# Down projection of an f32 encoder layer: pairs of k tiles, part of them by seven block products

## The chip, the core and the metric

The kernel runs on one core of a Trainium2 chip. The metric is device time in microseconds (us) for one execution of the whole layer; times given as "before" are of the unchanged kernel.

## The reference

One post-norm encoder layer on 256 tokens of width 2048, all in float32: a layer norm, one projection to 6144 columns, two kinds of attention over the 256 tokens, an output projection, and a gated feed-forward block of width 5632. What the change touches is the last line but one:

```
h = layer_norm(x, ln_in_g, ln_in_b)
proj = einsum('bsd,de->bse', h, w_in)                       # 2048 -> 6144, split in six
mixed = einsum('bse,ed->bsd', concat([na_out, diff_out]), w_out)
h = layer_norm(ALPHA * h + mixed, ln1_g, ln1_b)
ffn = einsum('bsf,fd->bsd', silu(h @ w_gate) * (h @ w_up), w_down)   # w_down: 5632 x 2048
h = layer_norm(ALPHA * h + ffn, ln2_g, ln2_b)
```

## The kernel before

**Arithmetic.** Each f32 matrix product is made of three matmuls in the format fp32r: every operand x is split in hi (x rounded, an ACTIVATE of ScalarE) and lo (x minus hi, a subtraction of VectorE), and the product is hi*hi + hi*lo + lo*hi. So each 128 x 1024 tile of weights costs one load (512 KB, SyncE's queue), one split on ScalarE and one on VectorE, and TensorE's matmuls are 128 x 128 by 128 x 512.

**Stages.** The work is a list of units, one tile of 128 rows (k) of a weight matrix and 1024 columns each. In order: six groups of 16 units for w_in; two groups of 16 for w_out ("o", 0 and 1); one chunk of 512 gate and up columns ("f", 10); five times a group "g" (gate) and a group "u" (up) of 16 units, for 1024 columns each; and ("d", 0) and ("d", 1), 44 units each, for the two halves of w_down's columns. The tokens are two tiles of 128, t = 0 and 1.

**Two kinds of steps.** Most groups go unit by unit: `mm_step(t, u)` (line 379) adds 6 matmuls for one token tile into two accumulators, a PSUM bank of 128 x 512 each. The groups g and u go by pairs of units. A pair is a 2 x 2 block matrix (two k tiles by two column halves of 512) times the 2 x 2 blocks of the tokens, so 8 block products of 3 matmuls each. In four of the eight pairs of a group (`SEVEN`) only 7 block products are taken, on sums of the blocks, in the manner of Strassen and Winograd: `seven_parts` (line 946) makes the sums of the weights (four adds of 512 columns on VectorE) and splits them, and `more_forms` (line 540) makes the sums of the tokens once, when layer norm 1 ends, since all ten groups use the same tokens. `products` (line 1008) lists the block products with their accumulators, 1 to 7; `take_product` (line 1055) issues them and reads accumulators out at the group's end.

**The down projection before** goes unit by unit, each unit 12 matmuls, 1056 in all, with four accumulators open at a time. Its left operand mid, silu(gate) * up, is transposed block by block (`mid_side`, line 905: four transposes of TensorE, a copy by ScalarE into the ring nb of two buffers, a store of 256 KB by GpSimd's queue to mid_d in HBM), read back as chunks of four k tiles (512 KB) and split (`mid_hi`, `mid_lo`, lines 914 and 918). The last eight units' part for t = 1 is kept for the end (`last_steps`, line 1248): those 48 matmuls run while the normalization of t = 0 is finished.

**What sets the order.** All engines' programs are written once, on the host, by a planner. `Timed` (line 63) keeps a clock for each engine and a time for each piece of a tile; before each step the planner looks at a window of coming steps (20 for products, 7 for others), and emits the splits and sums whose inputs its clocks call ready (`next_part`, line 1290); attention, norms and transposes are side tasks that are let in where the clocks see room (`Side`, line 177). Tiles of 4 KB a partition come from one pool of 46 slots (`slot`, line 267); PSUM banks come from `Banks` (line 140). Each engine runs its program in order, and waits at an instruction until the engines or DMAs it depends on have got there. All instructions are recorded by one helper, so the profile puts them on one line, L50.

Of the kernel before, what the change touches and what calls it, by code (L numbers as in the profile page):

```python
# [37 lines left out]
SEVEN = (0, 2, 4, 6)  # L38

# [23 lines left out]
class Timed:  # L63
# [32 lines left out]
    def note(self, name, op, outs, ins):  # L96
# [4 lines left out]
        if op == "dma_start":  # L101
# [5 lines left out]
            if name == "pool":  # L107
                end += 2.0
# [20 lines left out]
        self.clock[name] = end  # L129
        for w, r, c in map(self.times, ins):  # L130
            r[c] = np.maximum(r[c], end)
        for w, r, c in map(self.times, outs):
            w[c] = end + self.LATENCY[name]
# [6 lines left out]
class Banks:  # L140
# [30 lines left out]
    def next_idle(self):  # L171
        if self.count < 8:
            return 0.0
        return min([self.nc.idle(b) for b in self.left + self.passing], default=0.0)
# [73 lines left out]
def layer_kernel(ctx: ExitStack, tc: tile.TileContext, A: dict, out: bass.AP):  # L248
# [16 lines left out]
    slots = dict(used=0, left=[])  # L265

    def slot(shape, dt=F32):
        t = slab.tile(shape, dt, tag="slab", name=nm("sl"))
        if slots["used"] < SLOTS:
            slots["used"] += 1  # L270
        elif slots["left"]:
            old = min(slots["left"], key=lambda x: nc.idle(x))
            slots["left"].remove(old)
            nc.follows(t, old)
        return t

    def leave(*tiles):

        slots["left"] += tiles
# [33 lines left out]
    def add_group(name, ks, srcs, lhs):  # L313
        for i, k in enumerate(ks):
            units.append(dict(group=name, k=k, first=i == 0, last=i == len(ks) - 1, srcs=srcs, lhs=lhs))
# [15 lines left out]
    for j in range(NSG):  # L331
        for name, w in (("g", W_G), ("u", W_U)):
            add_group((name, j), range(KT), [w[:, j * 1024 : (j + 1) * 1024]], h1T)
    for c in range(2 * NSG, NFC - 1):
        add_f(c)
    for n in range(2):
        add_group(("d", n), range(KF), [W_D[:, n * 1024 : (n + 1) * 1024]], mid)
# [6 lines left out]

    def load(u):
        if u >= U:
            return
        if u == U - KF - 10:
# [4 lines left out]
        if units[u]["group"] == ("d", 0) and units[u]["k"] % 4 == 0:  # L353
            c = units[u]["k"] // 4
            side.drain_until(lambda: have.get(("mid whole", c), 0) == 2)
            mid_whole[c] = slot([P, 2, 4, P])
            nc.sync.dma_start(mid_whole[c], mid_d[c * P : (c + 1) * P, :])
        r = slot([P, 1024])
# [20 lines left out]
    def mm_step(t, u):  # L379
# [14 lines left out]
        if t == 1:  # L394
            leave(hi, lo)

# [21 lines left out]
    AHEAD_S = 20  # L418
    NPRE = 7
    NPRE_S = 8  # L420

# [54 lines left out]
    def ln_side(key, t, g, b, store, tiles, n_whole):  # L476
# [10 lines left out]
        for c in range(4):  # L487
            while (key, t, c, "norm") not in have:
                yield None
            yield "pe", [chunk(h[t], c)]  # L490
# [34 lines left out]
    def part_split(key, t, c, f, parts, late):  # L525
# [7 lines left out]
        have[key, t, c] = 1  # L533

# [3 lines left out]
    hF, forms, halves = {}, {}, []  # L538

    def more_forms(i):  # L540
# [12 lines left out]
        else:  # L553
            n = 2
            f = ring("s", 4, (P, 4, P))
            nc.vector.tensor_tensor(f[:, :2], ab, cd, op=ALU.subtract)
        f = f[:, :n]
        if n == 4:
            parts = slot([P, 2, n, P], F32R)
        elif len(halves) % 2 == 0:  # L560
            halves.append(slot([P, 2, 2, 2, P], F32R))
            parts = halves[-1][:, 0]
# [88 lines left out]
    def setup():  # L651
# [14 lines left out]
        nc.vector.tensor_copy(diag, bk[:DF_H, :])  # L666
        diag_d = dram.tile([DF_H, 512], F32, name="diag_d")
# [10 lines left out]
        nc.vector.tensor_tensor(lp, lv[:, 0:4:2, :], lv[:, 1:4:2, :], op=ALU.mult)  # L678
        ls = const.tile([P, 2], F32, name="ls")
# [28 lines left out]
    def qk_side(name, t, nat):  # L708
        for n in range(2):
# [7 lines left out]
            have[name] = have.get(name, 0) + 1  # L717

# [45 lines left out]
    def diff_head(hd):  # L764
# [29 lines left out]
        for qt in range(2):  # L794
            for kt in range(2):
# [6 lines left out]
                )  # L802
        o = ring("o", 2)
# [45 lines left out]
    def na_head(hd):  # L849
# [36 lines left out]
        for kt in range(2):  # L886
# [6 lines left out]
            )  # L893
        j = hd // 4
# [8 lines left out]
    mid_whole = {}  # L903
# [13 lines left out]

    def mid_lo(c):
        hi, lo = mid_tiles[c]
        nc.vector.tensor_tensor(lo, mid_whole[c], hi.bitcast(F32), op=ALU.subtract)  # L920
        leave(mid_whole[c])
# [11 lines left out]
    def op(engine, fn, reads=(), after=()):  # L933

        return dict(engine=engine, fn=fn, reads=reads, after=after, done=False)

    def one_parts(u):
# [6 lines left out]
        return [op("act", lambda: split_hi(u), lambda: [raw[u]]), op("dve", lo, lambda: [wh[u]], (0,))]  # L944

    def seven_parts(u):
# [23 lines left out]
        def lo13():  # L970
            nc.vector.tensor_tensor(s["lo"], s["t"], s["hi"].bitcast(F32), op=ALU.subtract)

        def t24():
            s["u"] = slot([P, 2, 512])
            nc.vector.tensor_tensor(s["u"][:, 0], s["t"][:, 0], r2[:, 512:], op=ALU.add)
            nc.vector.tensor_tensor(s["u"][:, 1], s["u"][:, 0], r2[:, :512], op=ALU.add)

# [4 lines left out]
        def lo24():  # L982
            nc.vector.tensor_tensor(s[4], s["u"], s[2].bitcast(F32), op=ALU.subtract)
            leave(s["u"], s["t"])

        def lo2():
            split_lo(u + 1)
            leave(r2)

        return [  # L990
            op("act", hi11, lambda: [r1]),
# [432 lines left out]
```

## Time and profile before

| | us |
|---|---|
| median of 3 runs (1129.63 to 1130.07) | 1130.06 |
| the profiled execution | 1130.14 |
| span of the profiled execution | 1128.2 |
| TensorE busy in the span | 1116.9 |
| VectorE busy | 848.6 |
| ScalarE busy | 569.9 |
| down projection, first matmul to its last accumulator | 875.5 to 1116.5 |

Times in rows are counted from the start of the span. PE is TensorE, PEld its weight loads, DVE VectorE, ACT ScalarE, POOL GpSimd, SP SyncE. "busy" counts an engine's instructions; idle time before an instruction stands in brackets, with what ended it. A tile's name in a row is that of the program without its number: sl is a slot, acc a PSUM bank, nb the ring of copies, s and o other rings.

### The profile page before, as it was taken

The numbers are of one execution on the slowest core, as the hardware profiler recorded it, in microseconds if no ns is written. First come the engines' busy times: TensorE is split into PE (matmuls) and PEld (weight loads), VectorE is DVE, ScalarE is ACT, GpSimd is POOL, SyncE is SP. The second block draws the span as 40 slices with busy tenths as digits, with TensorE's granted clock in tenths as the row PEclk, the third lists the DMA queues.
The fourth block names the chain that finished last, engine by engine and source line by source line (L and its number), as shares of the span: only waits on it lengthen the run. The fifth ranks groups of instructions, "written<-read, shape, count | busy, mean of one in ns | idle before, by whom it ended". The sixth has DMA issues, their size and how long they took to land.

```text
span 1128.2 us, 13969 instructions
## 1 busy us (share of the span) xinstructions
PE 1116.9 (99%) x5064; PEld 911.8 (81%) x5064; DVE 848.6 (75%) x1110; ACT 569.9 (51%) x740; POOL 60.3 (5%) x111
## 2 busy tenths in 40 slices
PE   8999999999999999999999999999999999999997
PEld 4788887888888867888888888888888888888885
DVE  7863867446774579899999999999999663455435
ACT  5552556325474236655566566555656543435420
POOL 2000003020100020000000000000000000000001
PEclk9999999999999999999999999999999999999999
DMA  9865548697857764564765766755757976567621
GB/s 328 274 186 157 158 149 178 210 180 187 180 166 276 239 195 153 184 219 170 249 214 189 246 205 216 227 191 210 238 190 277 350 248 240 183 244 234 224 67 74
DMA packets 68611, 234.24 MB, mean 208 GB/s; under 512 B 8388, under 2 KB 8516, under 8 KB 68544
## 3 DMA queue, kind: packets, MB, share of 16 engines
q1 hardware_dynamic: 63216, 217.61, 57.4%
q0 software_dynamic: 5168, 15.68, 7.1%
q8 instruction: 39, 0.64, 0.2%
q14 instruction: 28, 0.23, 0.1%
q10 hardware_dynamic: 160, 0.08, 0.0%
HBM read 223.36 MB, written 9.97 MB: 207 GB/s over the span
## 4 chain that ended last, share of the span: by engine, by line
PE 95%; DVE 2%; ACT 1%; POOL 1%; DMA 0%; issue 0%; POOLq 0%; ACTq 0%; DVEq 0%
PE acc L50 95%; DVE sl L50 2%; ACT sl L50 0%; DMA ident<-in_c_ident_dram 0%; POOL rs L50 0%; DVE stats L50 0%; POOL rstd L50 0%; DVE s L50 0%; ACT o L50 0%; DVE o L50 0%; ACT L50 0%; POOLq L1420 0%; DVE mv L50 0%; ACT nb L50 0%; ACT rows L50 0%
## 5 line engine op out<-in xcount | busy, mean ns | idle before, releaser
L50 PE MATMUL acc<-sl,sl 128*128 128x512 f32 (+1 forms) x4712 | 1068.8, 387 | 0.6 <-DVE sl L50 0.6
L50 PEld LDWEIGHTS acc<-sl,sl 128*128 128x128 f32 x4712 | 868.1, 188 | 181.0 <-issue 6.8
L50 DVE TENSOR_TENSOR sl<-sl,sl 128x1024 fp32r<-128x1024 f32 (+2 forms) x611 | 624.2, 1075 | 105.6 <-ACT sl L50 58.5
L50 ACT ACTIVATE sl<-sl 128x1024 fp32r<-128x1024 f32 (+1 forms) x491 | 470.9, 1011 | 264.7 <-DVE sl L50 132.5
L50 ACT ACTIVATE sl<-acc 128x256 fp32r<-128x256 f32 (+2 forms) x70 | 33.4, 499 | 112.5 <-PE acc L50 97.5
L50 DVE TENSOR_TENSOR sl<-acc,sl 128x256 fp32r<-128x256 f32 (+2 forms) x92 | 53.4, 594 | 30.4 <-ACT sl L50 27.6
L50 DVE SCALAR_TENSOR_TENSOR sl<-sl,acc 128x512 f32<-128x512 f32 x16 | 10.9, 679 | 58.3 <-PE acc L50 58.3
L50 DVE TENSOR_SCALAR sl<-acc 128x512 f32<-128x512 f32 x8 | 5.5, 688 | 50.4 <-PE acc L50 50.4
L50 POOL DMA_DIRECT2D mid_d<-nb x22 | 11.9, 542 | 458.4 <-ACT nb L50 458.4
L50 ACT COPY nb<-acc 128x512 f32<-128x512 f32 x24 | 14.1, 589 | 39.6 <-PE acc L50 31.9
L50 ACT COPY sl<-acc 128x512 f32<-128x512 f32 x28 | 15.4, 590 | 32.6 <-PE acc L50 32.5
L50 DVE TENSOR_TENSOR sl<-sl 128x512 f32<-128x512 f32 x40 | 27.4, 686 | 0.0
L50 ACT ACTIVATE s<-s 128x512 f32<-128x512 f32 x20 | 12.4, 634 | 29.2 <-DVE s L50 29.2
L50 POOL DMA_DIRECT2D nb<-in_na_rpb_dram x32 | 19.7, 623 | 95.0 <-DVE s L50 87.6
L50 ACT ACTIVATE s<-s,mx 128x256 f32<-128x256 f32 x32 | 15.9, 502 | 12.0 <-DVE mx L50 11.9
L50 PEld LDWEIGHTS acc<-ident,sl 128*128 128x128 f32 x128 | 15.1, 140 | 6.9 <-issue 3.7
L50 PE MATMUL acc<-ident,s 128*128 128x128 f32 x136 | 19.8, 272 | 0.0
L50 PEld LDWEIGHTS acc<-ident,s 128*128 128x128 f32 x136 | 16.6, 140 | 3.8
L50 DVE SCALAR_TENSOR_TENSOR sl<-sl,rstd,sl 128x512 f32<-128x512 f32 x22 | 16.5, 752 | 4.0 <-POOL rstd L50 3.1
L50 DVE BATCH_NORM_STATS2 stats<-sl 128x6 f32<-128x512 f32 x24 | 16.3, 691 | 2.9 <-DMA sl<-in_x_dram 2.4
L50 DVE SCALAR_TENSOR_TENSOR sl<-sl,mv,sl 128x512 f32<-128x512 f32 x24 | 17.7, 746 | 0.3
L50 ACT ACTIVATE rows<-ident,rstd 128x128 f32<-128x128 f32 x1 | 0.4, 403 | 34.3 <-POOL rstd L50 34.3
(76 smaller groups left out, 222.2 us busy)
## 6 DMA issues: line engine op xcount, KB each, us to landing
sl<-in_w_in_dram SPq DMA_DIRECT2D x96, 512.0 KB, 4.8
sl<-in_w_down_dram SPq DMA_DIRECT2D x88, 512.0 KB, 4.7
sl<-in_w_gate_dram SPq DMA_DIRECT2D x80, 512.0 KB, 4.6
sl<-in_w_up_dram SPq DMA_DIRECT2D x80, 512.0 KB, 4.4
sl<-in_w_out_dram SPq DMA_DIRECT2D x32, 512.0 KB, 5.6
mid_d<-nb POOLq DMA_DIRECT2D x22, 256.0 KB, 4.6
sl<-mid_d SPq DMA_DIRECT2D x11, 512.0 KB, 5.6
sl<-in_w_gate_dram SPq DMA_DIRECT2D x16, 256.0 KB, 4.1
```

The lines of the kernel that those rows point to most:

```text
L50: result = getattr(self.engine, op)(*args, **kw)
```

## The change

- The down projection goes by pairs. `SEVEN_D` names the pairs that take seven block products: 0, 3, 6, 9, 12, 15, 18 of the first group, and 20, 17, 14, 11, 8 of the second, which now takes its k tiles in reverse order of pairs. Plain pairs write accumulators 2, 3, 4 and 8, the others 1 to 7; all eight are open through most of a group. `down_ends` reads 1, 5, 6 and 7 out into h behind the last pair that uses them.
- Each of the twelve pairs makes the sums of its weights, and sums of its tokens (`add_mid_sums`: four subtractions of 128 columns and one split of 512 on VectorE, one split of 512 on ScalarE).
- In the second group three chunks of mid (`AGAIN`) are loaded and split again, and five half chunks of 256 KB are loaded for the sums of tokens. h is read back at unit 24 of the first group, and the gains of the last norm at unit 22 of the second.
- The planner counts slots (`room`): a split that takes a slot must leave six free if its step isn't among the next ones, loads wait for room too; its window is 24 steps for every kind; its clocks know the latency of a DMA and of a read; a product needs only those sums that it reads (`NEEDS`), not all of its pair.
- The last eight units' block products on accumulators 4 and 8 are kept for the end, 48 matmuls as before.

```diff
-AHEAD_S = 20
+AHEAD_S = 24
+SEVEN_D = (range(0, 20, 3), range(20, 5, -3))
+AGAIN = 3
+KEPT = 6
...
     for n in range(2):
-        add_group(("d", n), range(KF), [W_D[:, n * 1024 : (n + 1) * 1024]], mid)
+        ks = range(KF) if n == 0 else [k + i for k in range(KF - 2, -1, -2) for i in range(2)]
+        add_group(("d", n), ks, [W_D[:, n * 1024 : (n + 1) * 1024]], mid, SEVEN_D[n])
...
+        if is_down(u):
+            return [
+                (2, a_, b(0, 0)),
+                (2, b_, b(1, 0)),
+                (3, a_, b(0, 1)),
+                (3, b_, b(1, 1)),
+                (4, c_, b(0, 0)),
+                (4, d_, b(1, 0)),
+                (8, c_, b(0, 1)),
+                (8, d_, b(1, 1)),
+            ]
...
+    def down_ends(n, left, m):
+        if not any(x in left for x in (1, 5, 6, 7)) and 1 in q:
+            e = slot([P, 2, 512])
+            nc.scalar.copy(e[:, 0], q[1])
+            nc.vector.tensor_tensor(e[:, 1], q[6], e[:, 0], op=ALU.subtract)
+            scaled_into(0, 0, q[1], ALU.add)
+            for t, half, op in ((0, 1, ALU.add), (1, 1, ALU.add), (1, 0, ALU.subtract)):
+                scaled_into(t, half, e[:, 1], op)
+            into(0, 1, q[5], ALU.add)
+            into(1, 1, q[5], ALU.add)
+            into(1, 1, q[7], ALU.add)
+            into(1, 0, q[7], ALU.subtract)
+            for x in (1, 5, 6, 7):
+                banks.give(q.pop(x))
+        if m not in left and m in (2, 3, 4, 8):
+            t, half = {2: (0, 0), 3: (0, 1), 4: (1, 0), 8: (1, 1)}[m]
+            into(t, half, q[m], ALU.add, True)
+            banks.give(q.pop(m))
...
+                if o["takes"] and room() < o["takes"] + (0 if p in near else KEPT):
+                    continue
...
-            while loaded <= until:
+            while loaded <= until and (loaded <= self.top + 3 or self.kind != "product" or room() > KEPT + 2):
...
-        window = order[i : i + (AHEAD_S if step.kind == "product" else AHEAD)]
+        window = order[i : i + AHEAD_S]
```

The longer window also moves instructions in stages that the change doesn't rewrite. Three places follow. In the rows "[waits ...]" names what the instruction waits for; the number behind a tile's name only tells tiles apart and differs between the two programs.

ScalarE at the start, before: behind the last copies of the layer norm's gains come the two copies of transposed tokens into nb, then the splits of transposed tokens (from acc) and of weights (from sl).

```order
L50 COPY sl_137<-acc_176 128x512 [waits PE_49]
L50 COPY nb_205<-acc_200 128x512 [waits PE_49]
L50 COPY nb_227<-acc_222 128x512 [waits DVE_49,PE_49]
L50 ACTIVATE sl_229<-acc_231 128x4x128 [waits PE_49]
L50 ACTIVATE sl_248<-acc_250 128x4x128 [waits PE_49]
L50 ACTIVATE sl_263<-sl_94 128x1024 [waits DMAHW6_49]
```

The same place now:

```order
L52 COPY sl_137<-acc_176 128x512 [waits PE_49]
L52 ACTIVATE sl_198<-sl_94 128x1024 [waits DMAHW6_49]
L52 COPY nb_207<-acc_202 128x512 [waits PE_49]
L52 COPY nb_216<-acc_211 128x512 [waits DVE_49,PE_49]
L52 ACTIVATE sl_233<-sl_96 128x1024 [waits DMAHW0_49]
L52 ACTIVATE sl_235<-sl_102 128x1024 [waits DMAHW5_49]
```

The split of weight tile sl_94 moved from behind the first token splits to ahead of the first copy into nb; four more weight splits moved ahead of the token splits.

VectorE after layer norm 1, before: the last token sums (s) and splits of the first two chunks, then the run of weight splits (128x1024).

```order
L50 TENSOR_TENSOR s_3625<-sl_3528 128x256
L50 TENSOR_TENSOR sl_3591<-s_3586,sl_3591 128x512 [waits Activation_49]
L50 TENSOR_TENSOR sl_3600<-s_3598,sl_3600 128x256 [waits Activation_49]
L50 TENSOR_TENSOR sl_3521<-sl_3528,sl_3520 128x4x128
L50 TENSOR_TENSOR sl_3531<-sl_3538,sl_3530 128x4x128
L50 TENSOR_TENSOR sl_3654<-sl_3544,sl_3652 128x1024 [waits DMAHW4_49,DMAHW3_49,Activation_49]
L50 TENSOR_TENSOR sl_3661<-sl_3334,sl_3577 128x1024
L50 TENSOR_TENSOR sl_3668<-sl_3357,sl_3602 128x1024 [waits DMAHW6_49,DMAHW5_49]
```

The same place now, behind the sums of the first two chunks:

```order
L52 TENSOR_TENSOR sl_3678<-sl_3574,sl_3643 128x1024 [waits DMAHW4_49,DMAHW3_49]
L52 TENSOR_TENSOR sl_3642<-s_3637,sl_3642 128x512 [waits PE_49,Activation_49]
L52 TENSOR_TENSOR s_3688<-sl_3556 128x256
L52 TENSOR_TENSOR sl_3561<-sl_3568,sl_3560 128x4x128 [waits Activation_49]
L52 TENSOR_TENSOR s_3691<-sl_3568 128x128 [waits DVE_49]
L52 TENSOR_TENSOR s_3691<-sl_3568 128x128
L52 TENSOR_TENSOR s_3691<-sl_3568,s_3691 128x128 [waits DVE_49] x2
L52 TENSOR_TENSOR s_3702<-sl_3568 128x256
L52 TENSOR_TENSOR sl_3580<-sl_3587,sl_3579 128x4x128 [waits Activation_49]
L52 TENSOR_TENSOR s_3706<-sl_3587 128x128 x2
L52 TENSOR_TENSOR s_3706<-sl_3587,s_3706 128x128 [waits DVE_49] x2
L52 TENSOR_TENSOR sl_3723<-sl_3593,sl_3654 128x1024 [waits DMAHW5_49,DMASW6_49,DMAHW6_49,DMASW5_49,PE_49]
```

The sums of the third and fourth chunk moved ahead of the weight splits; of those, most stand before the norm now, and sl_3723 is the second that is left.

TensorE at the start of the down projection, before: transposes (ident) of the last gate/up block between products on four open accumulators.

```order
L50 MATMUL acc_7676<-ident,s_7270 128x128 [waits DVE_49]
L50 MATMUL acc_7676<-ident,s_7270 128x128 x3
L50 MATMUL acc_7648<-sl_7538,sl_7521 128x512
L50 MATMUL acc_7649<-sl_7538,sl_7521 128x512
L50 MATMUL acc_7648<-sl_7540,sl_7521 128x512
L50 MATMUL acc_7649<-sl_7540,sl_7521 128x512
L50 MATMUL acc_7648<-sl_7538,sl_7522 128x512
L50 MATMUL acc_7649<-sl_7538,sl_7522 128x512
L50 MATMUL acc_7690<-ident,s_7273 128x128 [waits DVE_49,Activation_49]
L50 MATMUL acc_7690<-ident,s_7273 128x128 x3
L50 MATMUL acc_7698<-ident,s_7282 128x128 [waits DVE_49]
L50 MATMUL acc_7698<-ident,s_7282 128x128 x3
```

The same place now:

```order
L52 MATMUL acc_7695<-sl_7557,sl_7576 128x512 [waits DVE_49]
L52 MATMUL acc_7695<-sl_7558,sl_7576 128x512
L52 MATMUL acc_7695<-sl_7557,sl_7576 128x512
L52 MATMUL acc_7701<-ident,s_7277 128x128 [waits DVE_49]
L52 MATMUL acc_7701<-ident,s_7277 128x128 x3
L52 MATMUL acc_7709<-sl_7569,sl_7576 128x512 [waits Activation_49]
L52 MATMUL acc_7709<-sl_7570,sl_7576 128x512
L52 MATMUL acc_7709<-sl_7569,sl_7576 128x512
L52 MATMUL acc_7715<-ident,s_7286 128x128 [waits DVE_49,Activation_49]
L52 MATMUL acc_7715<-ident,s_7286 128x128 x3
L52 MATMUL acc_7723<-sl_7569,sl_7513 128x512 [waits Activation_49]
```

Each block product now opens another bank between the transposes, and acc_7723, the seventh accumulator, waits for ScalarE's copy out of a transposed block's bank.

## Rows read from the trace of the kernel before

**Rows 1.** The page's busy times and its slices of DMA share, in tenths.

```profile
PE 1116.9 (99%) x5064; PEld 911.8 (81%) x5064; DVE 848.6 (75%) x1110; ACT 569.9 (51%) x740; POOL 60.3 (5%) x111
...
DMA  9865548697857764564765766755757976567621
```

**Rows 2.** Busy time in slices of 28.2 us; the first line names the columns.

```profile
core 0: us, PE busy (x) PEld busy (x) DVE busy (x) ACT busy (x) POOL busy (x), PEclk, DMA share, GB/s
...
169.20:197.40 28.20, 26.84 (x140) 22.46 (x139) 20.37 (x28) 17.33 (x34) 10.03 (x20) 1.00 0.82 178
...
507.60:535.80 28.20, 28.20 (x126) 23.37 (x125) 28.10 (x33) 16.91 (x19) 0.00 (x0) 1.00 0.50 171
...
874.20:902.40 28.20, 28.20 (x134) 23.41 (x133) 19.38 (x22) 15.88 (x19) 2.17 (x4) 1.00 0.91 350
```

**Rows 3.** Timeline of TensorE, the start: begin, duration, instructions, idle time before.

```profile
12.39 1.98 PE L50 MATMUL acc<-sl,nb 128*128 128x512 f32 x4 [0.77 <-ACT nb L50]
14.22 1.04 PE L50 MATMUL acc<-ident,sl 128*128 128x128 f32 x8
```

**Rows 4.** Groups by form: count, then busy us, mean ns of one, idle before.

```profile
L50 PE MATMUL acc<-sl,sl 128*128 128x512 f32 x4520 | 1047.0, 392 | 0.6 <-DVE sl L50 0.6
...
L50 PE MATMUL acc<-ident,sl 128*128 128x128 f32 x128 | 17.6, 273 | 0.0
```

**Rows 5.** Timeline of VectorE in the first gate/up group.

```profile
440.63 0.50 DVE L50 TENSOR_TENSOR s<-sl 128x128 f32<-128x128 f32 x2
441.03 0.62 DVE L50 TENSOR_TENSOR s<-sl,s 128x128 f32<-128x128 f32 x2
441.57 0.42 DVE L50 TENSOR_TENSOR s<-sl 128x256 f32<-128x256 f32 x1
441.91 0.69 DVE L50 TENSOR_TENSOR sl<-sl,sl 128x512 fp32r<-128x512 f32 x1
442.51 0.49 DVE L50 TENSOR_TENSOR s<-sl 128x128 f32<-128x128 f32 x2
...
448.79 1.22 DVE L50 TENSOR_TENSOR sl<-sl,sl 128x1024 fp32r<-128x1024 f32 x1
449.93 0.42 DVE L50 TENSOR_TENSOR sl<-s,sl 128x256 fp32r<-128x256 f32 x1
```

**Rows 6.** Timeline of all engines around layer norm 1.

```profile
399.31 0.69 DVE L50 SCALAR_TENSOR_TENSOR sl<-sl,acc 128x512 f32<-128x512 f32 x1 [15.81 <-PE acc L50]
...
418.45 1.29 DVE L50 TENSOR_TENSOR sl<-sl,sl 128x512 fp32r<-128x512 f32 x2
...
426.21 4.14 PE L50 MATMUL acc<-sl,sl 128*128 128x512 f32 x17 [0.57 <-DVE sl L50]
```

**Rows 7.** Timeline of all engines at the start of the down projection.

```profile
875.49 4.38 PE L50 MATMUL acc<-sl,sl 128*128 128x512 f32 x18
...
876.65 0.54 POOL L50 DMA_DIRECT2D mid_d<-nb  x1 [72.00 <-ACT nb L50]
...
888.28 0.59 ACT L50 COPY nb<-acc 128x512 f32<-128x512 f32 x1 [5.09 <-DMA mid_d<-nb]
888.77 17.19 ACT L50 ACTIVATE sl<-sl 128x1024 fp32r<-128x1024 f32 x18
...
889.86 15.99 DVE L50 TENSOR_TENSOR sl<-sl,sl 128x1024 fp32r<-128x1024 f32 x14 [8.72 <-ACT sl L50]
```

**Rows 8.** DMA view from 870 to 900: KB each, median us to landing.

```profile
mid_d<-nb POOLq DMA_DIRECT2D x4, 256.0 KB, 6.1
```

**Rows 9.** The tile mid_d, its 22 stores of the whole execution.

```profile
DMA to landing us min/median/max: 2.3/4.6/7.0
```

**Rows 10.** Timeline of TensorE in the tail.

```profile
1120.60 3.55 PE L50 MATMUL acc<-sl,rows 128*128 128x512 f32 x4 [2.38 <-ACT rows L50]
```

**Rows 11.** Busy time in slices of 2 us in the tail, columns as in rows 2.

```profile
1120.00:1122.00 2.00, 1.40 (x2) 0.58 (x3) 1.86 (x3) 0.40 (x1) 0.11 (x1) 0.72 0.12 45
1122.00:1124.00 2.00, 2.00 (x3) 0.34 (x1) 0.97 (x2) 0.59 (x1) 0.00 (x0) 0.50 0.26 96
```

## What is predicted

> **What bounds the kernel now.** I read the page first, then the busy time by slices, then the pauses of TensorE in the timeline, and last the places where the order changes. TensorE is busy 99% of the span, VectorE 75%, ScalarE 51% [rows 1]. In the slices TensorE fills 28.20 of 28.20 us in nearly all, at a granted clock of 1.00; a slice with a pause, 169.2 to 197.4, still shows 26.84 [rows 2]. So the time is the count of matmuls times their pitch, plus a few pauses. The pitch: 17 matmuls from 426.21 last 4.14 us [rows 6], and one alone is modelled at 0.39 us [rows 4], so (4.14 - 0.39) / 16 = 0.234; over a full slice it is 28.20 / 126 = 0.224 [rows 2]. I use 0.227, between them. In the gate/up slice 507.6 to 535.8 VectorE is busy 28.10 of 28.20, yet TensorE doesn't pause [rows 2]: VectorE keeps up there with nothing to spare. In the first slice of the down projection VectorE has 19.38 us of work [rows 2]. The change spends that room.
>
> **What is saved.** A plain pair of k tiles takes 8 block products of 3 matmuls, a seven-product pair 7. Twelve pairs lose 3 matmuls each: 36 x 0.227 = **-8.17 us**. The order shows 4468 wide matmuls for 4504, all other matmuls and the transposes as before. TensorE has no pause in the down projection to absorb this, so the gain is on the path. The 48 matmuls kept for the end, behind which the first token tile's normalization is hidden, are still 48, and the tail after them keeps its steps: 0.
>
> **The start.** ScalarE's first copy into nb sets TensorE's first f32 product at 12.39, after a pause of 0.77 us [rows 3]. In the new order a split of a weight tile stands ahead of that copy. Eighteen such splits from 888.77 take 17.19 us [rows 7], 0.95 each. TensorE then starts 0.95 later; four transposes that followed now go into the pause and give back 0.4 (eight last 1.04 us, one 0.27 of it [rows 3, 4]: (1.04 - 0.27) / 7 = 0.11 each). **+0.6**, between 0 (if the tile isn't the one waited for) and 1.0.
>
> **Layer norm to gate/up.** VectorE idles 15.81 us before the norm at 399.31 [rows 6]; about six weight splits move into that hole, at no cost, since it is twice as long as they. One split moves between the two token tiles (1.14, [rows 5]), and all token sums for the block products now stand ahead of the weight splits. TensorE asks early for one of those splits, sl_3723 in the order. VectorE's own chain to it: it begins at 418.45 [rows 6], plus the moved split 1.14, plus 8 subtractions of 512 columns x 0.60, 4 operations of 256 x 0.34, 4 pairs of 128 at 0.40 and 4 dependent pairs at 0.54, and 2 splits x 1.14 (starts to starts in [rows 5]): 12.2, so 431.8. TensorE came to the same place 18 matmuls behind 426.21 [rows 6], at 430.3, and that start already held a pause of 0.57. **+1.45** net; if the loads and splits run early enough, the 0.57 goes too: -0.6. Behind that place VectorE is ahead by more than before, since the splits in the hole are done; in the groups that follow I add no wait on it.
>
> **Block ends in gate/up.** Four times a bank is asked for again 6 matmuls (1.36 us) behind the transposes that filled it, where it was 9 or more. ScalarE's copy of it takes 0.59 [rows 7], and 0.95 more if a split is running. One wait in four: **+0.4**, between 0 and 1.4.
>
> **The start of the down projection.** The eight accumulators are all eight banks. The last gate/up block is still being transposed, through ScalarE's copies into the ring nb, two buffers deep, each freed when its store to mid_d has landed. Before, four accumulators were open and nobody waited for the copies: the fourth sat 5.09 us on a store, until 888.28, while TensorE ran on [rows 7]. Now the product on accumulator 4 (acc_7723 in the order) waits for the third copy's bank, so TensorE inherits that wait. The first store is issued at 876.65 [rows 7]; a store in this stretch lands 6.1 us later in the median [rows 8], 2.3 to 7.0 over all 22 [rows 9]. Landing 882.75, copy 0.6, TensorE released at 883.4. It gets there from 875.49 [rows 7] behind 18 matmuls (4.1) and three blocks of four transposes (0.44 each): 880.9. **+2.5**, between 0 (2.3 us) and 3.4 (7.0 us). The eighth accumulator waits for the fourth copy, whose store is issued by 879.8: landing 885.9 to 886.8, copy done by 887.4. TensorE arrives 21 matmuls after 883.4, at 888.2. No second pause.
> The Trainium skill ("DMA: Bandwidth & Descriptors", Anatomy of one DMA) gives a transfer on this path as a fixed 2.0 us plus bytes over 436 GB/s. By that estimate 256 KB lands after 2.6 us and this term is 0, the sum 1124.3; the trace's median here disagrees, since weight loads fill the queues.
>
> **Elementwise work of the down projection.** A seven-product pair costs VectorE 5 x 0.60 + 3 x 1.14 = 6.4 for the weights and 0.40 + 0.54 + 0.60 = 1.5 for the token sums, 8.0 in all; a plain pair two splits, 2.3; each two pairs share a mid split, 1.1 [rows 5]. From pair 3 to pair 18 of the first group that is 6 x 8.0 + 10 x 2.3 + 8 x 1.1 = 80 us. ScalarE is held by the fourth copy until 886.5, and all splits queue behind it, as 8.72 us of idle VectorE show already now [rows 7]. TensorE begins pair 3 at 883.4 + 51 x 0.227 = 895 and needs 366 x 0.227 = 83 us: it ends pair 18 at 978. VectorE has 92 us for 80. Cost 0, the narrowest margin about 2 us at pair 3, where ScalarE must do six splits and the sums' split first (6.2 us from 886.5). In the second group five pairs cost 40 us, of 117: 0. Evacuation (1 copy, 9 reads of banks) runs beside the 24 matmuls of the last pair. The eight more loads of mid_d are 2.8 MB, 8 us at the 350 GB/s of the first slice [rows 2]; the DMA queues are at 5 to 7 tenths further on [rows 1], so they fit: 0.
>
> **Sum.** -8.17 + 0.6 + 1.45 + 0.4 + 2.5 = -3.2. The profiled execution took 1130.14, the median is 1130.06, so 0.08 under it: **1126.8**. With each term at its better end it is 1130.06 - 8.17 - 0.6 = 1121.3; with each at its worse 1130.06 - 8.17 + 1.0 + 1.45 + 1.4 + 3.4 = 1129.1. A measurement of this kernel can tell about 0.2% (2.3 us) from no change, so faster means under 1127.8.
>
> **Rivals.**
> - *All covered.* The planner's new clocks serve: the store lands in 2 to 3 us and VectorE comes early to sl_3723. Then only the start's 0.6 stays: **1122.5**. For: the shortest landing is 2.3 [rows 9]. Against: that was in no stretch as full as this one.
> - *The pause at the down projection costs clock too.* Near the end TensorE pauses 2.38 us [rows 10], and the granted clock then shows 0.72 and 0.50 for two stretches of 2 us [rows 11], of which 0.50 is the lower level, 1.2 GHz. If the new pause of 2.5 us did the same, (0.28 + 0.50) x 2 = 1.6 us are lost on top: **1128.4**. Against: the slice with 1.36 us of pause kept 1.00 [rows 2].
> The Trainium skill ("TensorE: Matmul & The Clock Gate", Part 1) says that the throttled clock is the default and activity releases it; the tail's rows agree.
> - *Small pauses all over.* The planner's rules changed (slots counted, longer window, DMA latency), so the order moved everywhere, and what was just in time may not be. Before, the pauses shown here come to 2.7 us (0.77, 0.57, and 28.20 - 26.84 = 1.36 [rows 2, 3, 6]); as much again is +2.5 or so: **1129.3**, up to 1131 with a wait on the eighth bank.
> - *VectorE becomes the bound of the first down group* (the slow side). Place: pairs 3 to 18. It must be busy 80 of 92 us, 87%. In the slice in which this stretch begins it was busy 19.38 of 28.20, 69%, for want of ScalarE [rows 2, 7]. At 69% the 80 us take 116, 24 more than there are: **1150**; it costs from 87% down, and the kernel is slower than before from 82%. Against: with the same kind of pairs, four of eight, it ran at 28.10 of 28.20 [rows 2].
> - *The change does less than it says*: excluded, as the order has the 36 matmuls fewer.
>
> **How the numbers follow.** Forecast 0.50 (four fifths of it under 1127.8), all covered 0.17, clock 0.06, small pauses 0.17 (three quarters within 0.2%, the rest slower), VectorE 0.10 (mostly slower). Faster: 0.40 + 0.17 = 0.57. Slower: 0.04 + 0.08 = 0.12. Same: 0.31. The range reaches from the covered case, 1122, to the upper end of the small pauses, 1131; beyond lie VectorE's case and the edges.
>
> **What would show it.** Right: 36 matmuls fewer; TensorE's first f32 product near 13.3; one pause of 1 to 2 us on VectorE near 430; one of 2 to 3 us near 881 on a copy into nb, and no other in the down projection; its 1020 matmuls in about 232 us without pauses. Wrong: VectorE at 95% or more behind 895 with TensorE waiting for it; a granted clock under 1.00 near 884; load issues waiting for slots; pauses inside the gate/up groups that weren't there.

## The result, and the profile after

The changed kernel takes 1138.36 us in the median of four runs (1136.97 to 1141.19), the kernel before 1129.92 in the same rounds: a ratio of 1.0078, 95% interval 1.0056 to 1.0100. It is slower by 8.4 us; the forecast was 1126.8, 3.3 faster. The profiled execution took 1139.54 us with a span of 1137.7.

The page of after, busy times (before: [rows 1]):

```profile
PE 1113.4 (98%) x5028; PEld 906.4 (80%) x5028; DVE 932.1 (82%) x1263; ACT 601.2 (53%) x781; POOL 60.3 (5%) x111
```

TensorE's busy time fell (1116.9 to 1113.4) while the span grew by 9.5, so most of the time went into its pauses. Timeline of TensorE in after, from several stretches; the brackets give the idle time before and what ended it (before: [rows 3, 6, 7, 10]):

```profile
12.62 0.66 PE L52 MATMUL acc<-ident,sl 128*128 128x128 f32 x4 [0.86 <-DVE sl L52]
13.44 1.98 PE L52 MATMUL acc<-sl,nb 128*128 128x512 f32 x4 [0.15 <-ACT nb L52]
...
180.81 0.85 PE L52 MATMUL acc<-ident,o 128*128 128x128 f32 x4 [0.91 <-DVE o L52]
...
184.59 0.94 PE L52 MATMUL acc<-ident,o 128*128 128x128 f32 x4 [1.54 <-DVE o L52]
...
263.92 0.66 PE L52 MATMUL acc<-ident,sl 128*128 128x128 f32 x4 [1.77 <-ACT sl L52]
265.29 0.66 PE L52 MATMUL acc<-ident,sl 128*128 128x128 f32 x4 [0.72 <-DVE sl L52]
...
306.19 0.72 PE L52 MATMUL acc<-ident,s 128*128 128x128 f32 x4 [2.93 <-DVE s L52]
...
436.93 4.38 PE L52 MATMUL acc<-sl,sl 128*128 128x512 f32 x18 [0.40 <-DVE sl L52]
442.41 3.96 PE L52 MATMUL acc<-sl,sl 128*128 128x512 f32 x16 [1.10 <-DVE sl L52]
...
892.73 0.60 PE L52 MATMUL acc<-ident,s 128*128 128x128 f32 x4
896.99 8.27 PE L52 MATMUL acc<-sl,sl 128*128 128x512 f32 x28 [3.66 <-ACT nb L52]
...
1130.65 2.14 PE L52 MATMUL acc<-sl,rows 128*128 128x512 f32 x4 [2.38 <-ACT rows L52]
```

The five pauses from 180 to 306 lie in w_in's groups and the attention, stages that the change doesn't rewrite and reaches only through the planner; they come to 7.9 us, where before shows 1.36 [rows 2]. Between them and the tail stand the small ones near 440 and the 3.66 us at the start of the down projection; behind that one, 1002 matmuls run without a pause. Two of the pauses also cost clock. Busy time in slices of 2 us (after the counts: granted clock, DMA share, GB/s):

```profile
306.00:308.00 2.00, 1.81 (x9) 1.57 (x10) 1.97 (x8) 0.00 (x0) 0.00 (x0) 0.91 0.25 96
308.00:310.00 2.00, 2.00 (x6) 1.54 (x6) 1.80 (x3) 0.16 (x1) 0.00 (x0) 0.50 0.25 70
310.00:312.00 2.00, 2.00 (x8) 1.59 (x7) 1.16 (x4) 2.00 (x6) 0.00 (x0) 0.74 0.56 203
...
897.00:899.00 2.00, 2.00 (x7) 1.62 (x8) 1.83 (x2) 0.35 (x1) 0.54 (x1) 0.79 1.06 377
899.00:901.00 2.00, 2.00 (x6) 1.51 (x6) 0.78 (x1) 2.00 (x3) 0.54 (x1) 0.50 1.00 399
901.00:903.00 2.00, 2.00 (x9) 1.64 (x8) 2.00 (x5) 2.00 (x4) 0.00 (x0) 0.86 0.27 104
```

Each time the clock is at the lower level, 1.2 GHz, for some 3 us. What that costs is (0.21 + 0.50 + 0.14) x 2 = 1.7 us at 897, (0.09 + 0.50 + 0.26) x 2 = 1.7 at 306. Behind the other pauses shown, up to 1.8 us and the 2.38 in the tail, it stayed at 1.00.

Where the time went, by the same events in both traces (start of each group's read-out, the first norm after attention, the first matmul of the down projection, the first matmul behind the tail's pause):

| stretch | predicted | measured |
|---|---|---|
| start, to 111 us | +0.6 | +0.6 |
| w_in, attention, w_out, to layer norm 1 (399.31 before, 409.85 after) | 0 | +9.9 |
| layer norm 1 to the first matmul of the down projection (875.49, 887.61) | +1.85 | +1.6 |
| pause at that start | +2.5 | +3.66, and 1.7 of clock |
| rest of the down projection | -8.17 | -7.4 |
| tail | 0 | -0.6 |

The last but one is what is left: the tail's pause ends at 1130.65 instead of 1120.60, so 10.05 - 12.12 - 3.66 - 1.7 = -7.4. Of the 9.9, 7.9 - 1.36 are pauses. The rest is longer busy time: between the same transposes (113.49 to 406.14 before, 114.17 to 416.68 after) 1426 matmuls are busy 291.29 us before and 294.51 after, 3.2 more, of which the clock takes 1.7. Four transposes right behind a pause last 0.66 to 0.94 where the others last 0.60, which is part of the other 1.5.

Which engine was late in the attention? The rows show the waits of after: the engine and what it waited for, then us in all, times, longest. The kernel before has 4.2, 2, 4.0 for the first, and no row for the last two.

```profile
ACT sl L52 <- DMA sl<-in_w_in_dram: 42.9, 27, 6.9
ACT sl L52 <- DMA sl<-in_w_out_dram: 35.5, 20, 10.9
...
DVE s L52 <- DMA nb<-in_na_rpb_dram: 15.3, 5, 4.8
```

ScalarE's timeline in after, then in before, from 240 us, the end of a w_in group:

```profile
241.01 1.06 ACT L52 ACTIVATE sl<-sl 128x1024 fp32r<-128x1024 f32 x1 [6.95 <-DMA sl<-in_w_in_dram]
...
251.97 1.06 ACT L52 ACTIVATE sl<-sl 128x1024 fp32r<-128x1024 f32 x1 [5.95 <-DMA sl<-in_w_in_dram]
...
262.32 1.06 ACT L52 ACTIVATE sl<-sl 128x1024 fp32r<-128x1024 f32 x1 [0.21 <-DMA sl<-in_w_in_dram]
263.29 0.58 ACT L52 ACTIVATE sl<-acc 128x512 f32<-128x512 f32 x1
```

```profile
239.09 1.06 ACT L50 ACTIVATE sl<-sl 128x1024 fp32r<-128x1024 f32 x1 [1.20 <-PE acc L50]
256.99 0.60 ACT L50 ACTIVATE sl<-acc 128x512 f32<-128x512 f32 x1 [16.84 <-PE acc L50]
```

Before, ScalarE sat idle and read the accumulator out the moment TensorE had filled it, at 256.99. After, nine weight splits stand ahead of that read-out, each waiting for its own load, and it comes at 263.29, of whose delay 2.25 us is the shift that this group had already started with (222.45 instead of 220.20). TensorE's pause of 1.77 at 263.92 is this. The second pattern is on VectorE. The attention's eight heads take their biases (rpb) through a ring of two buffers, so each load is issued when VectorE has used the bias of two heads before. GpSimd's last two loads and VectorE's use of them, in after, then in before:

```profile
287.25 2.44 POOL L52 DMA_DIRECT2D nb<-in_na_rpb_dram  x4 [44.61 <-DVE s L52]
290.01 2.44 POOL L52 DMA_DIRECT2D nb<-in_na_rpb_dram  x4 [0.32 <-DVE s L52]
298.90 0.75 DVE L52 TENSOR_TENSOR s<-nb,cap 128x256 f32<-128x256 f32 x2
302.32 0.42 DVE L52 TENSOR_TENSOR s<-nb,cap 128x256 f32<-128x256 f32 x1
305.15 0.43 DVE L52 TENSOR_TENSOR s<-nb,cap 128x256 f32<-128x256 f32 x1 [2.42 <-DMA nb<-in_na_rpb_dram]
```

```profile
284.14 2.44 POOL L50 DMA_DIRECT2D nb<-in_na_rpb_dram  x4 [15.96 <-DVE s L50]
293.95 2.44 POOL L50 DMA_DIRECT2D nb<-in_na_rpb_dram  x4 [7.37 <-DVE sums L50]
306.05 0.75 DVE L50 TENSOR_TENSOR s<-nb,cap 128x256 f32<-128x256 f32 x2
318.28 0.75 DVE L50 TENSOR_TENSOR s<-nb,cap 128x256 f32<-128x256 f32 x2
```

The loads aren't what is late: the second to last comes 3.1 us later than before, which is about what the whole kernel is late by then, and the last one 3.9 us earlier. Nor are they slower: all 32 land 9.2 us after their issue in the median in both kernels, and 14.6 at most (15.0 before). What moved is their use. The last two heads stand earlier in the order, 12 us behind their loads instead of 22 and 24, and that is less than such a load can take. So VectorE waits 2.42 for one, and TensorE 2.93 for VectorE at 306.19. The profile's chain of the work that ended last runs through both patterns: 4.81 us of a load for w_in at 257.43 with its split at 262.32, and from 287.25 on 17.81 us of these two bias loads.

### The profile page after: what moved, and what is told of

It is laid out like the page before. It is cut to its first block, busy times and chain, and to the rows that moved or that the text cites. A ratio compares the mean times of both kernels' runs of the same rounds, so it can differ in the third digit from the quotient of the medians.

```text
span 1137.7 us, 14161 instructions
## 1 busy us (share of the span) xinstructions
PE 1113.4 (98%) x5028; PEld 906.4 (80%) x5028; DVE 932.1 (82%) x1263; ACT 601.2 (53%) x781; POOL 60.3 (5%) x111
## 4 chain that ended last, share of the span: by engine, by line
issue 40%; PE 30%; DMA 3%; DVE 2%; POOL 1%; ACT 1%; POOLq 0%; SPq 0%; ACTq 0%; DVEq 0%
PE acc L52 30%; DMA nb<-in_na_rpb_dram 2%; DVE sl L52 1%; DMA sl<-in_w_in_dram 1%; POOL mid_d L52 1%; DMA mid_d<-nb 1%; ACT sl L52 1%; ACT s L52 0%; POOL h_d L52 0%; DVE stats L52 0%; POOL rstd L52 0%; DVE s L52 0%; POOLq L1597 0%; DVE mv L52 0%; ACT nb L52 0%
## 5 line engine op out<-in xcount | busy, mean ns | idle before, releaser
L52 DVE TENSOR_TENSOR sl<-sl,sl 128x1024 fp32r<-128x1024 f32 (+3 forms) x710 | 685.4, 1016 | 75.3 <-ACT sl L52 65.1
L52 ACT ACTIVATE sl<-sl 128x1024 fp32r<-128x1024 f32 (+1 forms) x530 | 502.7, 995 | 311.3 <-DVE sl L52 113.7
L52 DVE TENSOR_TENSOR sl<-sl 128x512 f32<-128x512 f32 (+1 forms) x76 | 41.4, 557 | 3.9 <-PE acc L52 3.1
L52 PEld LDWEIGHTS acc<-ident,sl 128*128 128x128 f32 x128 | 14.9, 141 | 10.7 <-issue 3.6
L52 DVE TENSOR_TENSOR sl<-sl,acc 128x512 f32<-128x512 f32 x16 | 10.6, 680 | 13.6 <-PE acc L52 13.5
L52 PE MATMUL acc<-ident,sl 128*128 128x128 f32 x128 | 18.0, 275 | 3.5 <-ACT sl L52 1.8
L52 DVE TENSOR_TENSOR s<-nb,cap 128x256 f32<-128x256 f32 x16 | 6.2, 419 | 15.3 <-DMA nb<-in_na_rpb_dram 15.3
```

The lines of the kernel that those rows point to most:

```text
L52: result = getattr(self.engine, op)(*args, **kw)
```

## Experiments

Each was timed in rounds with the kernel before on the same chip; ratios are to that kernel, with the 95% interval. "Offset" is the time of an event minus that of the same event in the kernel before; "layer norm 1 is at +1.3" gives the offset of its first operation. An offset comes from the one profiled execution of each kernel. Four of the kernels below have the same window, clocks and slots ahead of layer norm 1, and theirs lie between +1.3 and +2.2, so a difference under 1 us says nothing.

**Which rule hurts the attention: the window.** The changed kernel, with the old window of 7 for everything but products:

```diff
-        window = order[i : i + AHEAD_S]
+        window = order[i : i + (AHEAD_S if step.kind == "product" else AHEAD)]
```

> The changed kernel, but with the planner's window for the steps outside the pairs (QKV, attention, output projection) back at 7 steps; the gate/up and down stages keep their order. Theory A (the long window puts weight splits, which wait for their loads, ahead of attention's copies on ScalarE): the 10.5 us by which layer norm 1 came later (399.3 to 409.9) go, pauses at 264 and 306 vanish, ScalarE's waits for w_in loads fall from 42.9 us to under 10; about 1128, 0.998 of before. Rival B (the loads are late by themselves, through the planner's other new rules on slots and DMA latency): the pauses stay within a third, 1135 or more. The pause of 3.7 us at the start of the down projection stays by both.

1130.63 us, ratio 1.0006 (0.9996 to 1.0016). Layer norm 1 is at +1.3 instead of +10.5, and ScalarE's waits for w_in fall from 42.9 to 14.2. One pause of 1.51 is left in the attention; the pause at the down projection's start stays, at 3.78, with a clock of 0.94 in that slice. So most of the loss hangs on the window here, but 2.6 us more than the expected 1128 are left.

**The start of the down projection.** The changed kernel, with the last two chunks' copies in slots instead of the two-deep ring:

```diff
-        f = ring("nb", 2, (P, 512))
+        last = c in (2 * NSG - 2, 2 * NSG - 1)
+        f = slot([P, 512]) if last else ring("nb", 2, (P, 512))
```

> The changed kernel, but the copies of the last two gate/up chunks go to slots of the pool instead of the ring of two buffers, so that no copy waits for a store to land; window still 24. Theory A (TensorE waited on the ring, and its clock fell for it): the pause of 3.66 us goes and with it about 1.7 us at the lower clock, 5.4 in all, 1133.0. Rival C (the clock falls there for another reason): 1134.7, and a granted clock under 1.00 near 897 stays. Rival D (VectorE is too late behind it): a new pause at pair 3, gain under 2 us, 1136.5 or more.

1133.79 us, 1.0033 (1.0021 to 1.0045), 4.6 under the changed kernel. Its timeline of TensorE, then the busy times of the slice:

```profile
892.83 0.60 PE L52 MATMUL acc<-ident,s 128*128 128x128 f32 x4
893.19 11.17 PE L52 MATMUL acc<-sl,sl 128*128 128x512 f32 x48
```

```profile
874.20:902.40 28.20, 28.20 (x134) 23.36 (x133) 27.64 (x40) 17.33 (x22) 2.16 (x4) 1.00 0.83 289
```

There is no pause, and the clock (third number from the end) keeps 1.00: the third copy did wait for the first store, and the pause did take the clock with it.

**Both together.** The edits of the first two experiments in one kernel.

> Both edits: window 7 outside the pairs, and slots for the last copies. If the two losses are separate they add: 1138.4 - 10.5 - 5.4 = 1122.5, 0.9934 of before, and what is left of TensorE's pauses is as before but for about 1 us behind layer norm 1. If the down projection is held by VectorE, or the loads are late by themselves, 1126 or more.

1125.89 us, 0.9963 (0.9950 to 0.9976), 3.4 above the 1122.5 that it would be if both losses went whole. Layer norm 1 is at +1.8, and the tail from the end of its pause on takes 8.1 us where the changed kernel takes 7.0 (its clock, see the last section); this accounts for 2.8 in the profiled executions. The pairs save about what was predicted: from the first matmul of the down projection to the tail's pause TensorE needs 237.56 us (878.83 to 1116.39) against 245.11, so -7.55 for 36 x 0.227 = 8.17. Busy times there, VectorE third:

```profile
882.00:900.00 18.00, 18.00 (x86) 14.95 (x85) 17.93 (x23) 13.47 (x16) 1.62 (x3) 1.00 0.92 337
900.00:915.70 15.70, 15.70 (x71) 12.98 (x70) 15.63 (x22) 7.08 (x8) 0.00 (x0) 1.00 0.74 253
915.70:931.40 15.70, 15.70 (x71) 13.00 (x70) 15.60 (x22) 10.98 (x12) 0.00 (x0) 1.00 0.85 312
...
947.10:962.80 15.70, 15.70 (x71) 13.01 (x70) 13.44 (x19) 8.80 (x11) 0.00 (x0) 1.00 0.52 161
962.80:978.50 15.70, 15.70 (x71) 12.97 (x71) 11.36 (x14) 8.47 (x10) 0.00 (x0) 1.00 0.70 237
```

VectorE is full at first, yet TensorE never pauses, and from 947 on VectorE has time to spare: with one pair in three it is full because it works ahead. The runs spread by 0.7 us (1125.72 to 1126.46), against 4.2 in the changed kernel. The store, which lands after 2.3 to 8.3 us in these traces, no longer reaches TensorE, but that alone isn't shown to be why: the second experiment, without that wait too, spread by 4.0 (1132.39 to 1136.34).

**Without the seven-product pairs.** The first experiment with `SEVEN_D = ((), ())`. With no such pair `down_ends` isn't reached: the residual is added without its factor, and accumulators 1, 5, 6 and 7 are not read out (1 copy, 9 reads).

> As the first of these runs (window 7), but all 44 pairs of the down projection by eight products, none by seven (SEVEN_D empty): 36 matmuls more, and four accumulators open at its start as before. Theory A (TensorE is the bound there, seven products save 0.227 us for each matmul, and cost only the bank wait): against the window run +8.2 for the matmuls and -5.4 for the pause and its clock, 1130.8. Rival D (VectorE's sums cost time in the down projection): as fast as or faster than the window run.

1132.88 us, 1.0025 (1.0015 to 1.0035): 7.0 above the version with twelve such pairs and no pause at the start. From layer norm 1 to the tail's pause it takes 722.86 us for 715.32, 7.5 more; its four matmuls behind that pause then last 2.14 for 3.68. The saving is real and close to its predicted 8.17.

**The planner's clocks.** On top of both, the old rules of `Timed` (no DMA latency, reads as before) wherever the step isn't a product, and with them the old answer of `Banks` when no bank is free (0.0 instead of 1e9):

```diff
-            self.clock["dma"] = end
-            end += self.LATENCY["dma"] + (2.0 if name == "pool" else 0.0)
+            if self.late:
+                self.clock["dma"] = end
+                end += self.LATENCY["dma"] + (2.0 if name == "pool" else 0.0)
...
-        window = order[i : i + AHEAD_S]
+        nc.late = step.kind == "product"
+        window = order[i : i + (AHEAD_S if step.kind == "product" else AHEAD)]
```

> The kernel with both edits (window 7 outside the pairs, slots for the last copies), and outside the pairs also the planner's old clocks (no DMA latency on its queue's clock, no latency on reads). It was 1125.9 without this. Theory A2 (what attention still loses, about 2 us between 262 and 361, comes from the new clocks' order): that falls under 0.7, 1124.5. Rival B2 (it comes from the new choice of slots, which stays): unchanged, 1125.9.

1123.27 us, 0.9941 (0.9926 to 0.9956). Layer norm 1 is at -0.6: the loss ahead of it is gone whole, and of the pauses there 0.60 at 181.74 is left.

**The window with the old clocks.** The same with 24 instead of 7.

> As the run with the old clocks, but the window outside the pairs at 24 again. Theory A (the long window alone makes ScalarE's program wait for loads): 8 to 10 us slower than that run, about 1133, and ScalarE's waits for w_in loads back over 30 us. Rival B3 (the window hurts only together with the new clocks): under 1127.

1126.46 us, 0.9968 (0.9956 to 0.9980). Layer norm 1 is at +3.5, and ScalarE waits 24.3 us for w_in: the window alone costs 4.0 here, not the 10 that it would if it were the whole cause.

**The window in the kernel before.** Window 24 for the units ahead of gate/up, nothing else changed.

> The kernel before with one number changed: the window outside the pairs and the down projection 24 instead of 7 steps. Theory A: 8 to 10 us slower than before, 1138 to 1140, pauses of TensorE at about 260 and 305. Rival B3: within 2 us of before.

1131.79 us, 1.0014 (1.0005 to 1.0023), layer norm 1 at -0.3. ScalarE waits 23.1 us for w_in, and yet nothing ahead of layer norm 1 is late for it. So the window by itself isn't the cause of that loss. It isn't free either: what this kernel loses, it loses behind layer norm 1. VectorE, TensorE and the busy times there:

```profile
418.10 7.50 DVE L50 TENSOR_TENSOR sl<-sl,sl 128x1024 fp32r<-128x1024 f32 x7
```

```profile
429.39 6.91 PE L50 MATMUL acc<-sl,sl 128*128 128x512 f32 x22 [2.05 <-DVE sl L50]
```

```profile
430.00:432.00 2.00, 2.00 (x6) 1.59 (x5) 2.00 (x6) 2.00 (x3) 0.00 (x0) 0.50 0.03 8
```

Seven splits, most of them of weights, stand on VectorE ahead of the token sums, which begin at 419.66 before and at 425.51 here. TensorE pauses 2.05 us for VectorE where it paused 0.57, and the clock falls behind it.

**The clocks in the kernel before**, alone, for the same units (here `Banks` keeps its old answer):

```diff
+            if self.early:
+                self.clock["dma"] = end
+                end += self.LATENCY["dma"]
```

> The kernel before with the new clocks alone outside the pairs and the down projection (window 7, old slots). With the new slots and window 7 the clocks cost 1.9 to 2.3 us (the run with both edits against the run with old clocks). If that is the clocks' own, layer norm 1 comes about 2 us late and the time is 1132; if it needs the new slots, 1130.

1136.55 us, 1.0054 (1.0037 to 1.0071), layer norm 1 at +6.1 where 2 was expected, with 3.9 us of waits for w_in. TensorE and the waits:

```profile
299.20 0.81 PE L50 MATMUL acc<-ident,s 128*128 128x128 f32 x4 [0.96 <-DVE s L50]
...
306.84 0.81 PE L50 MATMUL acc<-ident,s 128*128 128x128 f32 x4 [2.73 <-DVE s L50]
```

```profile
DVE s L50 <- DMA nb<-in_na_rpb_dram: 13.8, 5, 4.7
```

The clocks by themselves bring the last heads close behind their bias loads, as in the changed kernel. The traces of all the kernels agree: with the new clocks the last bias is used some 12 to 14 us after its load begins, and TensorE pauses on the heads' tiles (s) for up to 3.31 us; with the old clocks it is 24 to 26 us, and there is no such pause.

**Window and clocks in the kernel before:**

> The kernel before with window 24 and the new clocks outside the pairs and the down projection, but the old way with slots. By layer norm 1 the window alone cost nothing there (-0.3 us), window and new slots 3.5, all three 10.5. Theory A3 (clocks and window are what hurts, slots only add to it): 5 us or more late at layer norm 1, 1135 or more. Rival S (without the counted slots the loads come in time): under 2 us late, 1132 or less.

1134.61 us, 1.0044 (1.0028 to 1.0060), layer norm 1 at +2.75, between the two expectations. In the old slots the window seems to take back part of what the clocks cost ahead of layer norm 1, but the intervals of the two times overlap. ScalarE waits 45.9 us for w_in here, more than the 42.9 of the changed kernel, and TensorE's only pause on ScalarE from w_in to layer norm 1 is 0.48: the sum of an engine's waits doesn't tell what they cost TensorE. The offsets of layer norm 1 side by side:

| | window 7 | window 24 |
|---|---|---|
| slots as before, old clocks | 0 | -0.3 |
| slots as before, new clocks | +6.1 | +2.75 |
| slots counted, old clocks | -0.6, -0.2 | +3.5 |
| slots counted, new clocks | +1.3 to +2.2 | +10.5, +10.7 |

(Where there are several numbers, several kernels share that order.) No row or column is bad by itself, nor does the sum of single effects give 10.5 (from -0.6, the window adds 4.0 and the clocks 2.2: 5.6). What stands is that the two patterns, splits queued ahead of a read-out and heads queued close behind their bias loads, come from the order, that the second goes with the clocks, and that both go when window and clocks go back. Which other rule adds to them isn't separated: "slots counted" stands for every other rule that changed, and "clocks" takes in the answer of `Banks` in the lower rows only. Why they add up to 5 us more together stays open.

**How many such pairs VectorE carries.** The version with both cures, and in the second group every second pair instead of every third, eight instead of five:

```diff
-SEVEN_D = (range(0, 20, 3), range(20, 5, -3))
+SEVEN_D = (range(0, 20, 3), range(20, 5, -2))
```

> The kernel with both edits (1125.9), and three more pairs of the second down group by seven products: eight pairs, every second one, instead of five; 9 matmuls fewer. Theory A (TensorE is the bound of the down projection, VectorE has room): -2.0 for 9 x 0.227, 1123.9. Rival D (VectorE is near its bound there): 1125.5 or more, with pauses of TensorE behind 995.

1132.66 us, 1.0020 (1.0010 to 1.0030): 6.8 slower than with five, with 9 matmuls fewer. TensorE's timeline, then the busy times of one period, then ScalarE and VectorE at its start:

```profile
1013.12 10.77 PE L52 MATMUL acc<-sl,sl 128*128 128x512 f32 x45 [0.43 <-ACT sl L52]
1024.32 10.77 PE L52 MATMUL acc<-sl,sl 128*128 128x512 f32 x45 [0.42 <-ACT sl L52]
```

```profile
1013.12:1024.32 11.20, 10.78 (x46) 8.29 (x46) 10.37 (x16) 6.21 (x8) 1.04 (x2) 1.00 0.86 292
```

```profile
1012.44 2.53 ACT L52 ACTIVATE sl<-sl 128x512 fp32r<-128x512 f32 x3 [2.47 <-DVE sl L52]
1013.10 1.83 DVE L52 TENSOR_TENSOR sl<-sl,sl 128x512 fp32r<-128x512 f32 x2 [0.76 <-ACT sl L52]
```

A period of 45 matmuls takes 11.20 us where 45 x 0.227 = 10.2. VectorE is busy 10.37 of it, more than TensorE needs, and for most of the rest it waits for ScalarE, which waited for VectorE's sums. This is the rival in which VectorE becomes the bound: it is true at one pair in two and not at one in three.

**One more pair.** The version with old clocks and window 7, and `range(20, 4, -3)`, six pairs in the second group:

> The kernel with both edits and old clocks (1123.27), and pair 5 of the second down group by seven products as well, so six pairs there, still every third: 3 matmuls fewer, -0.7, 1122.6. Theory: one in three pairs is within VectorE's room (8.0 + 2 x 2.3 = 12.6 us of 69 matmuls, 15.7), as one in two was not (10.3 of 10.2). Rival: the extra work near the end delays the last pairs, 1123.3 or more.

1122.48 us, 0.9933 (0.9918 to 0.9948), 0.8 under five pairs, for 3 x 0.227 = 0.7; the two intervals overlap, so its lead over five pairs isn't certain. Its lead over the kernel before and over the changed kernel is.

## Why the prediction was wrong

- *What bounds the kernel*: right. TensorE was the bound, and the time came and went as matmuls, pauses and the clock behind pauses.
- *What is saved* (-8.17): right, a little large: -7.4 in the changed kernel, -7.55 and -7.5 in the experiments.
- *The start* (+0.6): the mechanism is right. TensorE's first f32 product came at 13.44, as the text put it near 13.3; in all five kernels with a split ahead of that copy it comes at 13.29 to 13.64, in the eight others at 12.38 to 13.08. That +0.6 is also what was left at 111 us is partly luck, since executions differ by more than that there: the eight reach the same transposes near 114 us at 113.49 to 114.37, the five at 113.95 to 114.24.
- *Layer norm to gate/up* (+1.45): right. With the shift of 10.5 us the estimate has TensorE go on at 442.3 behind 18 matmuls, and it did at 442.41, after pauses on VectorE of 0.40 and 1.10. This is nearly all of the +1.6 in the table.
- *Block ends in gate/up* (+0.4): not seen. TensorE has no pause between those and the down projection.
- *The start of the down projection* (+2.5): right mechanism, mis-sized. The first store was issued at 888.77, exactly where the estimate puts it with the shift of 12.1; TensorE ran out of work at 893.3 for an estimated 893.0. The landing was the miss: 7.5 us where the median row gave 6.1 [rows 8], past the 7.0 of [rows 9]. The second experiment shows the wait by taking it away. The Trainium skill's fit ("DMA: Bandwidth & Descriptors", Anatomy of one DMA), with 2.6 us by estimate for these 256 KB, would have had no pause at all: the trace disagrees, at 7.5.
- *The pause costs clock too* (rival, 0.06): this happened; 1.7 us measured for 1.6 worked out. It was weighed by a slice with 1.36 us of pause, when the pause forecast, 2.5, was nearer to the tail's 2.38.
- *VectorE becomes the bound* (rival): not in the changed kernel, where no product of the down projection waits behind 896.99. The margin was narrow, as the eight pairs show.
- *Small pauses all over* (rival, 0.17): this is the step that failed. The sum has no term between the start and layer norm 1, so it puts w_in, the attention and w_out at nothing, and gives no reason. The rival named the mechanism (rules for the planner's window, slots and latencies hold for the whole program), but its price was "as much again" as the 2.7 us of pauses before. That bounds nothing: a pause isn't a multiple of the old ones, it is what a changed order makes late. Measured, +9.9 ahead of layer norm 1, mostly in pauses from the two patterns and the clock that one of them cost. What a new order could make late could be named from the trace of before: read-outs that ScalarE did at once, and biases that were used 22 and 24 us behind their loads. The prediction costed neither.

With the attention's loss and the ring's wait taken out, as in the fifth experiment, the rest of the sum was good: -8.17 + 0.6 + 1.85 = -5.7 gives 1124.3, and 1123.27 was measured. In that order the start costs nothing (first f32 product at 12.44), which is part of the difference.

## What to carry to other kernels

A constant or a rule of a planner is a change to every stage that it plans: compare the order in the stages that aren't meant, and ask for each in-order engine what now stands ahead of the instruction that TensorE waits for, and how far behind its load each use stands. When a product comes to need all banks, the depth of the ring that empties them is on the path, and a store's landing there is the price: here 7.5 us, longer than any of the 22 stores before. Trading matmuls for elementwise work pays up to the share at which the helper engine's chain per period is shorter than TensorE's: here one pair in three, not one in two.

## What was not expected of the hardware

The same pause of 2.38 us in the tail cost clock in some profiled executions and not in others. Busy times of the tail with old clocks and window 7, and with one more pair:

```profile
1115.00:1117.00 2.00, 2.00 (x4) 0.66 (x2) 1.48 (x3) 0.59 (x1) 0.00 (x0) 0.50 0.35 131
```

```profile
1115.00:1117.00 2.00, 0.95 (x2) 0.12 (x2) 1.18 (x2) 1.14 (x2) 0.00 (x0) 1.00 0.63 231
```

The four matmuls behind it last 3.68 us in the one and 2.14 in the other; before had 3.55, the changed kernel 2.14 (the table's last row, -0.6, has this in it). The length of the pause alone doesn't decide. In the changed kernel pauses up to 1.8 us kept 1.00, and those of 2.93 and 3.66 lost it for some 3 us; 2.38 went both ways, the 2.05 at 429.39 in the kernel before with window 24 lost it, and the 2.73 at 306.84 in the kernel before with the new clocks kept 1.00:

```profile
308.00:310.00 2.00, 2.00 (x10) 1.65 (x9) 1.48 (x3) 2.00 (x6) 0.00 (x0) 1.00 0.05 20
```

So a difference of 1.5 us between two profiled executions can be the clock's alone. Each kernel has one profile, so whether this goes with the kernel or changes from one execution to the next isn't shown; the mean clocks of the unchanged kernel's executions lie between 0.996 and 1.000. What else decides, no run here was made to show. The Trainium skill ("TensorE: Matmul & The Clock Gate", Part 1) has the throttled clock as the default that activity releases; the falls behind 2.93 and 3.66 agree with that. It doesn't tell why the 2.73 kept the clock.
